# The first layer's MLP by 2x2 blocks in seven products

## The chip, the core and the metric

One NeuronCore of a Trainium2 chip runs the whole two-layer network in one launch. The metric is the device time of that launch in microseconds, the median of three runs. All arithmetic is fp32. A matrix product is split for TensorE: each operand is written as a high part (rounded to the format that TensorE multiplies) plus a low part (what is left), and three products are accumulated: high by high, high by low, low by high.

## The reference, cut to what matters

```python
for l in range(2):                       # D_MODEL 1024, D_FF 4096, 1024 latent + 256 context tokens
    ...                                  # projection, attention / convolution / Fourier heads, output projection
    x = layer_norm(ALPHA * x + g1 * mix_x, ln1_g[l], ln1_b[l])
    x = layer_norm(ALPHA * x + g2 * squared_relu_mlp(modulate(x, sh2, sc2), w_up[l], w_down[l]), ln2_g[l], ln2_b[l])
    if l == 0:
        ...                              # the same for ctx, with its own modulation vectors
def squared_relu_mlp(h, w_up, w_down):
    return jnp.square(jax.nn.relu(h @ w_up)) @ w_down
```

In the first layer latent and context tokens go through the MLP together, 1280 tokens; in the second only the 1024 latent ones do.

## The kernel before, in words

The program's order is written out by hand: each engine runs its own instructions in the order in which the Python code issues them, and waits only for data and for buffers. Loads and most stores of the MLP stand in one queue, that of SP (`load`, L193); the projections' stores stand in ScalarE's.

Buffers in SBUF: 25 tiles of 128x1280 (`s5`, tiles named a), 20 of 128x1024 (`s4`, b), two of 128x512 for the background stream's data (w) and four of 128x256 for its sums (m). A freed buffer goes to the end of a list, and a new tile takes the one that has been free longest. PSUM has eight banks of 512 columns: two tiles of three banks (`p3`, p) and two of one bank (`p1`, q).

`mm3` (L205 to L207) issues the three matmuls of one product tile. `lo` (L201) makes a low part, on VectorE or GpSimd.

Layer 0's MLP is `mlp_steps`. The hidden layer has 32 units of 128 columns. An up step `u(f)` multiplies one unit for all 1280 tokens, in chunks of 512, 512 and 256 columns: 24 matmuls each. ScalarE then makes Relu and Square (L1959, L1960), GpSimd the exact square (L1961) and VectorE the low part. A down step `d(j)` takes two units and all ten tiles of 128 tokens, two halves of 512 columns each, six matmuls a half, 120 in all, and VectorE adds the result to the sum in SBUF (L2025). The steps alternate: d, u, u, d, u, u. Units 0 and 1 are computed ahead, at the end of the output projection (`pre`). In the last down step the gate and the residual are folded into the sum (GpSimd L2043, VectorE L2046). Then comes unit 31, and `finish` does the last two units' down product with the layer norm, tile by tile (L2245).

A background stream (`stream`) is drawn on between steps: first `resid_jobs`, 20 jobs that make the residual from the stored layer-norm output (L1468, L1469), then `mod_jobs`, 16 jobs for each modulation vector that is still to come (L308, L310). A job loads 256 KB while its predecessor runs and gives two turns. Behind every fourth job stands a tail: a few small matmuls and one or two VectorE instructions on a PSUM tile. Three of the ten modulation vectors are made in `in_proj` of layer 0 (`NREST0`), the other seven in layer 0's MLP.

Layer 1's MLP is `mlp_blocks` and `down_blocks`. There the products go by 2x2 blocks in seven instead of eight products (Strassen's scheme in Winograd's form). Two units and two halves of the tokens make one pair `p`. The seven products are numbered; 1, 6, 7 and 4 accumulate in one PSUM bank, 5 and 3 in a second, 2 in a third, and between products ScalarE or VectorE reads the partial sum (`evac`, L1661 to L1674). The hidden blocks are summed (L1685), and all seven forms of them are stored to DRAM. The down phase loads them back, makes high and low parts (L1788, L1791, L201), multiplies by tiles of 128 tokens, and VectorE adds each product to the sum in SBUF (L1889). Four units are not in blocks: two done ahead, two `plain`. The token sums that the blocks need are made from fp32 copies of the MLP's input, which the output projection stores to DRAM in layer 1 (`XF`, in `to_T`). The second halves of `X2`, free by then, hold the weights' high and low parts.

Of the kernel before, what the change touches and what calls it, by code (L numbers as in the profile page):

```python
# [10 lines left out]
F32 = mybir.dt.float32  # L11
# [23 lines left out]
NREST0 = 3  # L35
# [110 lines left out]
class Prog:  # L146
    def __init__(self, nc, tc, a, out, pools):
        self.nc, self.tc, self.a, self.out = nc, tc, a, out
        self.cp, self.sp, self.ppc, self.dp = pools
        self.pp = self.ppc.__enter__()  # L150
        self.NP1 = 2
        self.n = 0
        self.wsrc, self.wrdy, self.wraw = [], [], []
# [14 lines left out]
    def s4(self, dt=F32, shape=(128, 1024)):  # L168
        return self.sp.tile(list(shape), dt, tag="s4", bufs=self.N4, name=self.nm("b"))
# [115 lines left out]
    def mod_jobs(self, idx):  # L285
# [5 lines left out]
        def job(q, kt):  # L291
            cs = slice(256 * q, 256 * q + 256)

            def load():
                w = self.sp.tile([128, 2, 256], F32, tag="mw", bufs=2, name=self.nm("w"))
# [4 lines left out]
            def run(w):  # L300
                if kt == 0:
                    acc[q] = {v: self.sp.tile([128, 256], F32, tag="ma", bufs=4, name=self.nm("m")) for v in vecs}
# [450 lines left out]
    def in_steps(self, X, l, PS):  # L753
# [11 lines left out]
        for i in range(NREST0) if l == 0 else ():  # L765
# [518 lines left out]
    def out_proj_setup(self, l):  # L1284
# [6 lines left out]
        self.XF = self.dr([KT, 128, SEQ]) if l else None  # L1291
# [154 lines left out]
    def resid_jobs(self, l, T):  # L1446
# [4 lines left out]
        def job(q, t):  # L1451
            cs = slice(512 * q, 512 * q + 512)

            def load():
                if q not in G:
                    G[q] = [[self.sp.tile([128, 256], F32, tag="ma", bufs=4, name=self.nm("m")) for _ in range(2)]
# [5 lines left out]
                w = self.sp.tile([128, 2, 256], F32, tag="mw", bufs=2, name=self.nm("w"))  # L1462
# [3 lines left out]
            def run(w):  # L1466
# [6 lines left out]
                self.nr -= 1  # L1473
# [4 lines left out]
    def mlp_seq(self, l):  # L1478
        seq = [("u", 0), ("u", 1), ("u", 2)]
        J = NFF // 2  # L1480
        for j in range(J - 1 - l):
            seq.append(("d", j))
            seq += [("u", f) for f in (2 * j + 3, 2 * j + 4) if f < NFF]
        if l:
            seq.append(("u", NFF - 1))
        return seq

    def mlp_push(self, l):
        self.WQ = 2
        if l:  # L1490
            for f in range(2 * NPL):
                self.wq_push(self.a["wu"][l, f], [128, KT, 128])
            return
# [7 lines left out]
    def mlp(self, X2, l):  # L1501
        with self.tc.manual_schedule():
            if l:
                self.mlp_blocks(X2, l)
            else:
                self.mlp_steps(X2, l)

    def mlp_blocks(self, X2, l):
# [186 lines left out]
        self.bank_pool()  # L1695
# [45 lines left out]
    def bank_pool(self):  # L1741
        self.ppc.__exit__(None, None, None)
        self.ppc = self.tc.tile_pool(name="pq", bufs=1, space=PSUM, reuse_waits="tile")
        self.pp = self.ppc.__enter__()
        self.NP1 = 8
# [623 lines left out]
```

## Time and profile before

| | |
|---|---|
| median of 3 runs | 2980.92 us (2979.51 to 2981.08) |
| the profiled execution, its span | 2984.5 us, 2982.5 us |
| busy: TensorE, VectorE, ScalarE, GpSimd | 95%, 63%, 33%, 33% |
| mean granted TensorE clock | 0.976 |
| layer 0's MLP, from unit 2 to the closing stage | 789.73 to 1650.68 us |

Times in the rows are from the span's start. PE is TensorE, PEld its weight loads, DVE is VectorE, ACT ScalarE, POOL GpSimd, SP the queue that issues most DMAs. A matmul's duration runs from its start to its modelled end, and successive ones overlap, so the rate is read from the distance of starts.

### The profile page before, as it was taken

To read this page: it belongs to the slowest core of one execution; us is meant where nothing else is said; L and a number is where in the kernel's file an instruction comes from. 1 tells how busy PE (TensorE), PEld (TensorE's weight loads), DVE (VectorE), ACT (ScalarE), POOL (GpSimd) and SP (SyncE) were. 2 spreads that over 40 slices of the span, in tenths; PEclk is the share of its full clock that TensorE was granted. 3 is DMA by queue.
4 is the path that set the end of the run, shared out by engine and by line. 5 is a ranking of instruction groups with operands and counts; after the bars stand their busy time and mean duration, and the time that the engine had idled before them with its cause. 6 is when DMAs were issued, how large, how long until landed. Compare 5 with 4: busy or idle time off the path is not lost. (4 is left out here: it accounts for less than half of the span.)

```text
span 2982.5 us, 36498 instructions
## 1 busy us (share of the span) xinstructions
PE 2821.0 (95%) x14164; PEld 2359.7 (79%) x14164; DVE 1890.7 (63%) x2725; ACT 997.4 (33%) x1364; POOL 986.9 (33%) x596
## 2 busy tenths in 40 slices
PE   7899989889999999999999899999989899999996
PEld 5788888778888878888887688888777788878875
DVE  6667768845345576655556743467855577668887
ACT  4221156523421111111111432146623555553331
POOL 2512135633211100000104640036655000058785
PEclk9999999999999999999999999999999999999998
DMA  7244652336223222223223223254345555464442
GB/s 258 82 158 135 188 131 68 103 132 215 85 85 111 78 91 90 89 82 98 80 88 124 113 87 134 94 163 94 109 146 191 176 206 196 149 232 156 155 151 96
DMA packets 197201, 389.16 MB, mean 130 GB/s; under 512 B 16702, under 2 KB 109348, under 8 KB 197028
## 3 DMA queue, kind: packets, MB, share of 16 engines
q1 hardware_dynamic: 176856, 315.47, 33.7%
q10 hardware_dynamic: 17292, 61.93, 5.4%
q0 software_dynamic: 2880, 9.44, 0.8%
q8 instruction: 111, 1.82, 0.3%
q14 instruction: 62, 0.51, 0.1%
HBM read 283.44 MB, written 103.34 MB: 130 GB/s over the span
## 5 line engine op out<-in xcount | busy, mean ns | idle before, releaser
L206 PE MATMUL p<-a,b 128*128 128x512 f32 (+1 forms) x1784 | 653.7, 366 | 1.1 <-POOL a L201 1.0
L205 PE MATMUL p<-a,b 128*128 128x512 f32 (+1 forms) x1512 | 552.1, 365 | 5.3 <-ACT b L1926 3.1
L207 PE MATMUL p<-a,b 128*128 128x256 f32 (+1 forms) x1496 | 539.2, 360 | 3.2 <-DVE b L201 3.1
L205 PE MATMUL q<-b,a 128*128 128x512 f32 (+1 forms) x1300 | 475.8, 366 | 27.9 <-ACT b L575 9.5
L206 PE MATMUL q<-b,a 128*128 128x512 f32 (+1 forms) x1300 | 469.2, 361 | 2.5 <-DVE b L201 2.5
L207 PE MATMUL q<-b,a 128*128 128x512 f32 (+1 forms) x1300 | 469.1, 361 | 0.1
L206 PEld LDWEIGHTS p<-a,b 128*128 128x128 f32 x1784 | 340.0, 191 | 52.3 <-POOL a L201 1.9
L205 PEld LDWEIGHTS p<-a,b 128*128 128x128 f32 x1512 | 287.6, 190 | 51.6 <-issue 6.2
L207 PEld LDWEIGHTS p<-a,b 128*128 128x128 f32 x1496 | 283.8, 190 | 47.8 <-DVE b L201 4.7
L205 PEld LDWEIGHTS q<-b,a 128*128 128x128 f32 x1300 | 248.5, 191 | 83.5 <-DVE b L2025 16.1
L2025 DVE TENSOR_TENSOR b<-q,b 128x512 f32<-128x512 f32 x280 | 192.6, 690 | 155.9 <-PE q L207 154.2
L206 PEld LDWEIGHTS q<-b,a 128*128 128x128 f32 x1300 | 248.5, 191 | 37.5 <-DVE b L201 3.1
L207 PEld LDWEIGHTS q<-b,a 128*128 128x128 f32 x1300 | 248.2, 191 | 37.5 <-DVE a L201 0.5
L201 DVE TENSOR_TENSOR b<-b,b 128x1024 fp32r<-128x1024 f32 (+1 forms) x119 | 181.4, 1532 | 150.4 <-ACT b L1926 119.1
L201 DVE TENSOR_TENSOR a<-a,a 128x1280 fp32r<-128x1280 f32 (+4 forms) x141 | 211.0, 1497 | 94.6 <-POOL a L1961 67.8
L1961 POOL TENSOR_TENSOR a<-a 128x1280 f32<-128x1280 f32 x31 | 72.0, 2322 | 585.6 <-ACT a L1960 585.6
L310 DVE SCALAR_TENSOR_TENSOR m<-w,k,m 128x256 f32<-128x256 f32 x448 | 226.4, 519 | 50.8 <-DMA w<-wmr 41.2
L201 POOL TENSOR_TENSOR a<-b,a 128x256 fp32r<-128x256 f32 (+2 forms) x133 | 176.8, 1339 | 241.9 <-ACT a L1791 126.1
L205 PE MATMUL q<-a,a 128*128 128x512 f32 x554 | 218.5, 394 | 14.7 <-DVE b L1889 13.1
L929 DVE TENSOR_REDUCE c<-p 128x1 f32<-128x1280 f32 x128 | 190.5, 1488 | 65.0 <-PE p L927 63.7
L207 PE MATMUL q<-a,a 128*128 128x512 f32 (+1 forms) x576 | 225.7, 392 | 0.2 <-DVE a L201 0.2
L206 PE MATMUL q<-a,a 128*128 128x512 f32 x568 | 223.7, 394 | 2.3 <-POOL a L201 2.3
(270 smaller groups left out, 4749.0 us busy)
## 6 DMA issues: line engine op xcount, KB each, us to landing
w<-wmr SPq DMA_DIRECT2D x160, 256.0 KB
a<-d SPq DMA_DIRECT2D x76, 512.0 KB
b<-wu SPq DMA_DIRECT2D x64, 512.0 KB
b<-wd SPq DMA_DIRECT2D x62, 512.0 KB
d<-a ACTq DMA_DIRECT2D x40, 640.0 KB
a<-d SPq DMA_DIRECT2D x80, 320.0 KB
d<-a SPq DMA_DIRECT2D x46, 512.0 KB
b<-wi SPq DMA_DIRECT2D x32, 512.0 KB
```

The lines of the kernel that those rows point to most:

```text
L201: (eng or self.nc.vector).tensor_tensor(out, x, hi, op=ALU.subtract)
L205: mm(out, lh, rh, start=start, stop=False, skip_group_check=on)
L206: mm(out, lh, rl, start=False, stop=False, skip_group_check=on)
L207: mm(out, ll, rh, start=False, stop=stop, skip_group_check=on)
L310: nc.vector.scalar_tensor_tensor(a, w[:, i], s, a, op0=ALU.mult, op1=ALU.add)
L929: nc.vector.reduce_max(mx, ps[:, :nkey], axis=AX.X, negate=True)
L1961: nc.gpsimd.tensor_tensor(r[:, s], r[:, s], r[:, s], op=ALU.mult)
L2025: nc.vector.tensor_tensor(a, ps, a, op=ALU.add)
```

## The change

Layer 0's MLP goes by blocks too, in a function of its own, `mlp_blocks0`, and in a common `down_blocks`. A token half has 640 columns there, so a product's moving operand is two parts of 320 columns, on a PSUM tile of two banks (`p2`, four of them). The order of the products differs from layer 1's. The down phase has five token tiles in each half, and all eight banks: five for the products 1, 6, 7 and 4, three for 5, 3 and 2. The two plain units' hidden values and those of units 0 and 1 are stored, and multiplied at the end: units 0 and 1 in `down_blocks`, 2 and 3 in `finish`. The pool of 128x1024 tiles is divided anew for the up phase: five `s4`, twelve 128x1280 tiles `t5`, and the stream's tiles; afterwards it has its 20 tiles again. Layer 0's output projection now stores `XF` too. Four of the modulation vectors (64 jobs, of one vector each) move from layer 0's MLP to `in_proj` of layer 1.

```diff
-NREST0 = 3
+NREST0, NREST1 = 3, 6
+BKU = {1: 2, 2: 1, 3: 1, 4: 2, 5: 1, 6: 1, 7: 2}
...
+    def p2(self):
+        return self.pp.tile([128, 2, 512], F32, tag="p2", bufs=4, name=self.nm("q"))
...
-        for i in range(NREST0) if l == 0 else ():
+        for i in range(NREST0) if l == 0 else range(NREST1, len(REST)):
             jobs += self.mod_jobs(i)
...
-        self.XF = self.dr([KT, 128, SEQ]) if l else None
+        self.XF = self.dr([KT, 128, SEQ if l else TOK])
...
+    def mlp_blocks0(self, X2, l):
...
+        self.sbuf(5)
+        self.anchor = self.last_load
+        jobs = self.resid_jobs(l, T)
+        for i in range(NREST0, NREST1):
+            jobs += self.mod_jobs(i)
+        bg = self.stream(jobs)
...
+        def plain_evac(f, ps):
+            r = self.t5()
+            act.activation(r, ps[:, :n], AF.Relu)
+            act.activation(r, r, AF.Square)
+            return lambda: self.load(self.HL[f], r)
...
+        def sum_split(k):
+            TS[k] = []
+            for j, x in enumerate(S1.pop(k)):
+                hi, lo = [(self.t5 if j and (k or i) else self.s5)(F32R) for i in range(2)]
+                act.copy(hi, x)
+                self.lo(lo, x, hi)
+                TS[k].append((hi, lo))
...
+        seq = [(NPL, 1), (NPL, 2)]
+        for p in range(NPL, NP):
+            seq += [(p, 5), (p, 6)] + [(p, 2)] * (p > NPL) + [(p, 7), (p, 3)]
+            seq += [(p + 1, 1)] * (p < NP - 1) + [(p, 4)]
...
+        def prod(n, o, start):
+            hi, lo = F.pop(n)
+            i = seq[n][1]
+            for h in range(2):
+                c = slice(Q2 * h, Q2 * h + Q2)
+                for k in range(4):
+                    xh, xl = B[i](k)
+                    self.mm3(o[:, h, :Q2], hi[:, k], lo[:, k], xh[:, c], xl[:, c], start and k == 0, k == 3, not start)
...
+        def evac(n):
...
+            if i in (1, 6):
+                act.copy(two(h["q"][:, int(i == 6)]), ps)
+            elif i == 7:
+                y = h["r"][:, 1]
+                act.copy(two(y), ps)
+                c = Q[p][5][:, :, :Q2]
+                return lambda: v.tensor_tensor(two(y), c, two(y), op=ALU.add), lambda: square(y)
+            elif i == 2:
+                y = h["q"][:, 0]
+                v.tensor_tensor(two(y), ps, two(y), op=ALU.add)
+            elif i == 4:
+                y = h["r"][:, 0]
+                act.activation(two(y), ps, AF.Relu)
+                Q.pop(p)
+                return None, lambda: act.activation(y, y, AF.Square)
+            elif i == 3:
+                y = h["q"][:, 1]
+                v.tensor_tensor(two(y), ps, two(y), op=ALU.add)
+            return None, None if y is None else (lambda: square(y))
...
+        st = [plain_evac(f, ready[f]) for f in range(2)]
+        pconv(2)
+        sum_load(0)
+        st.append(plain(2, {0: [P(sum_add, 0), P(pconv, 3)], 1: [st[0], P(sum_load, 1), P(sum_split, 0)],
+                            2: [st[1], P(wload, NPL), P(sum_add, 1)], 3: [P(sum_split, 1), P(sum_load, 2), back],
+                            4: [P(sum_add, 2), back], 5: [P(sum_split, 2), P(sum_load, 3)]}))
+        st.append(plain(3, {0: [P(sum_add, 3)], 1: [P(sum_split, 3), st[2], P(wload, NPL + 1)], 2: [back], 3: [back],
+                            4: [back], 5: [back]}))
+
+        self.psum(0)
...
+        for k, (p, i) in enumerate(seq):
+            q = Q.setdefault(p, {})
+            q[i] = q[{6: 1, 7: 1, 4: 1, 3: 5}[i]] if i in (6, 7, 4, 3) else self.p2()
+            prod(k, q[i], i in (1, 2, 5))
+            nxt = evac(k)
+            whi(k + 3)
+            wlo(k + 2)
+            if nxt[0]:
+                nxt[0]()
+            wsum(k + 4)
+            if post:
+                post()
+            post = nxt[1]
...
+            if i == 6 and p > NPL:
+                hstore(p - 1)
+            if i == 3:
+                wload(p + 2)
+            if i == 7:
+                tail()
+            if i == 4:
+                tail()
+            back(BKU[i])
+            if p == NP - 1 and i in (2, 7, 3):
+                next(down)
+        post()
...
     def down_blocks(self, l, NG):
...
+        order, steps = ((1, 5, 6, 3, 2, 7, 4), [(i, t) for i in (1, 5, 6, 3, 2, 7, 4) for t in al]) if l else (
+            (1, 5, 3, 6, 2, 7, 4),
+            [(i, t) for i, ts in ((1, al), (5, (0, 1, 2)), (3, (0, 1, 2)), (5, (3, 4)), (6, (0, 1)), (3, (3, 4)),
+                                  (6, (2, 3, 4)), (2, al), (7, al), (4, al)) for t in ts])
...
+        def where(i, t):
+            if i in (1, 6, 7, 4):
+                return "x", t
+            if l:
+                return "y", t
+            return "y", (t % 3 if i != 2 else (t + 2) % 3)
...
+        tasks = {0: [P(hraw, 2), P(wl, 2)], 1: [P(wl, 3)], 2: [hconv, P(hraw, 3)], 3: [wm], 4: [hconv], 5: [wm],
+                 T - 1: [P(fold_late, T + i) for i in range(FL)]}
+        for t in range(T):
+            c = slice(128 * t, 128 * t + 128)
+            for m in range(2):
+                ps = (bk["x"] + bk["y"])[(2 * t + m) % 8]
+                evac(2, ps)
+                d = slice(NB * m, NB * m + NB)
+                for e in range(2):
+                    self.mm3(ps, H[e][0][:, c], H[e][1][:, c], W[e][0][:, d], W[e][1][:, d], e == 0, e == 1)
+                evq.append((acc[t][:, d], ps, False))
+            evac(0)
+            fold_late(t)
+            for f in tasks.get(t, ()):
+                f()
...
-    def mlp_steps(self, X2, l):
...
-        wraw(NFF - 2)
-        wraw(NFF - 1)
+        wraw(2)
+        wraw(3)
```

`whi` and `wlo` make a weight block's high part (ScalarE) and low part (VectorE), `wsum` the sum of two blocks (VectorE), `hsums` the four sums of hidden blocks (VectorE), `back` takes one turn of the background stream, and `tail` one step of a modulation tail.

## Rows read from the trace of the kernel before

**Rows 1.** The page, part 1: busy time, share of the span, instructions.
```profile
PE 2821.0 (95%) x14164; PEld 2359.7 (79%) x14164; DVE 1890.7 (63%) x2725; ACT 997.4 (33%) x1364; POOL 986.9 (33%) x596
```
**Rows 2.** Table by stage: window, length, busy time by engine, clock, DMA share, GB/s.
```profile
789.73:1650.68 860.95, 852.89 (x4093) 704.81 (x4092) 505.76 (x830) 148.92 (x145) 122.41 (x65) 1.00 0.29 91
1597.92:1650.68 52.76, 45.43 (x201) 35.92 (x200) 40.91 (x36) 6.96 (x8) 41.66 (x15) 0.97 0.39 133
1655.00:1682.00 27.00, 18.94 (x81) 12.77 (x80) 26.24 (x40) 10.13 (x10) 15.10 (x11) 1.00 0.24 96
2327.00:2340.00 13.00, 9.82 (x34) 7.30 (x33) 8.88 (x11) 5.96 (x6) 0.00 (x0) 0.74 0.88 334
2375.00:2580.00 205.00, 202.68 (x889) 166.42 (x889) 141.22 (x250) 106.72 (x190) 8.79 (x16) 1.00 0.56 191
1740.00:2000.00 260.00, 252.40 (x1471) 223.52 (x1470) 122.93 (x112) 69.68 (x86) 48.66 (x28) 0.99 0.37 120
```
**Rows 3.** Instructions in order of time, layer 0's MLP, TensorE: start, duration, operation.
```profile
858.94 0.40 PE L205 MATMUL q<-b,a 128*128 128x512 f32 x1
...
886.54 0.39 PE L205 MATMUL p<-a,b 128*128 128x512 f32 x1
...
897.42 0.28 PE L205 MATMUL p<-a,b 128*128 128x256 f32 x1
...
900.29 0.40 PE L205 MATMUL p<-a,b 128*128 128x512 f32 x1
```
**Rows 4.** Groups by line, VectorE, layer 1's up phase: count, busy, mean ns, idle before.
```profile
L201 DVE TENSOR_TENSOR a<-b,a 128x512 fp32r<-128x512 f32 x52 | 35.5, 685 | 1.6 <-ACT a L1634 1.2
...
L1469 DVE TENSOR_TENSOR w<-w,m 128x256 f32<-128x256 f32 x31 | 13.2, 425 | 1.1
...
L1674 DVE TENSOR_TENSOR a<-q,a 128x512 f32<-128x512 f32 x11 | 7.6, 692 | 27.5 <-PE q L207 27.5
```
**Rows 5.** Groups by line, VectorE, layer 0's MLP.
```profile
L310 DVE SCALAR_TENSOR_TENSOR m<-w,k,m 128x256 f32<-128x256 f32 x280 | 132.6, 483 | 35.7 <-DMA w<-wmr 29.6
...
L201 DVE TENSOR_TENSOR a<-a,a 128x1280 fp32r<-128x1280 f32 x27 | 40.2, 1488 | 67.8 <-POOL a L1961 67.8
```
**Rows 6.** Groups by line, ScalarE, layer 1's up phase: a copy from PSUM.
```profile
L1661 ACT COPY a<-q 128x512 f32<-128x512 f32 x22 | 13.0, 589 | 25.2 <-PE q L207 25.2
```
**Rows 7.** Groups by line, ScalarE, layer 0's MLP: Relu from PSUM.
```profile
L1959 ACT ACTIVATE a<-p 128x1280 f32<-128x1280 f32 x28 | 34.8, 1242 | 322.1 <-PE p L207 322.1
```
**Rows 8.** In order of time, layer 1's last pair, product 7 and 4 behind it.
```profile
2623.37 0.39 PE L207 MATMUL q<-b,a 128*128 128x512 f32 x1
2623.80 0.59 ACT L1663 COPY a<-q 128x512 f32<-128x512 f32 x1 [3.81 <-PE q L207]
...
2624.44 0.50 PE L205 MATMUL q<-b,a 128*128 128x512 f32 x1 [0.68 <-ACT a L1663]
```
**Rows 9.** In order of time, start of layer 1's MLP, TensorE.
```profile
2327.23 0.28 PE L207 MATMUL p<-a,b 128*128 128x256 f32 x1
2330.65 0.79 PE L205 MATMUL p<-a,b 128*128 128x512 f32 x1 [3.14 <-ACT b L1926]
...
2358.26 0.50 PE L205 MATMUL q<-a 128*128 128x512 f32 x1 [2.71 <-ACT a L1634]
```
**Rows 10.** In order of time, layer 1, first down product, TensorE.
```profile
2631.73 0.49 PE L205 MATMUL q<-a,a 128*128 128x512 f32 x1 [1.55 <-ACT a L1791]
...
2634.31 0.79 PE L206 MATMUL q<-a,a 128*128 128x512 f32 x1 [2.08 <-POOL a L201]
```
**Rows 11.** Groups by line, VectorE, layer 1's down phase.
```profile
L201 DVE TENSOR_TENSOR a<-a,a 128x1024 fp32r<-128x1024 f32 x34 | 67.1, 1973 | 2.4 <-ACT a L1788 2.4
```
**Rows 12.** In order of time, end of layer 0's MLP: GpSimd's folds, first closing add.
```profile
1621.66 16.64 POOL L2043 TENSOR_TENSOR b<-b,b 128x1024 f32<-128x1024 f32 x5 [1.34 <-DVE b L2025]
...
1651.58 0.69 DVE L2245 TENSOR_TENSOR b<-q,b 128x512 f32<-128x512 f32 x1 [1.20 <-PE q L207]
```
**Rows 13.** Groups by line, VectorE, in_proj of layer 0.
```profile
L310 DVE SCALAR_TENSOR_TENSOR m<-w,k,m 128x256 f32<-128x256 f32 x152 | 83.6, 573 | 14.7 <-DMA w<-wmr 11.6
```

More of the change, by code (lines that the diff above doesn't have):

```diff
@@ L1455, in load @@
                 if q not in G:
-                    G[q] = [[self.sp.tile([128, 256], F32, tag="ma", bufs=4, name=self.nm("m")) for _ in range(2)]
+                    G[q] = [[self.ma() for _ in range(2)]
                             for _ in range(2)]
@@ L1505, in mlp @@
             else:
[L1506 removed]
+                self.mlp_blocks0(X2, l)
     def mlp_blocks(self, X2, l):
@@ L1753, in down_blocks @@
         seq = [(n, i) for n in range(NG) for i in order]
+        prods = [(n, i, t) for n in range(NG) for i, t in steps]
         acc = [None] * T
@@ L1819, in loads_to @@
                 pos[0] += 1
-        for k in (2, 4, 5):
-            loads_to(k)
-            yield
+        if l:
+            for k in (2, 4, 5):
+                loads_to(k)
+                yield
+        else:
+            for k in (3, 4):
+                loads_to(k)
+                yield
         f = form(*seq[0])
@@ L1830, in down_blocks @@
         yield
-        loads_to(7)
+        loads_to(7 if l else 6)
         for _ in form(*seq[1]):
             pass
-        bk = {b: [self.p1() for _ in range(4)] for b in "xy"}
-        W, H, S = [], [], []
+        self.psum(8)
+        bk = {"x": [self.p1() for _ in al], "y": [self.p1() for _ in range(8 - TH)]}
+        W, H, S, HR = [], [], [], []
         xr = {}
         self.acc = acc
+        gate = lambda t: self.gs[int(t >= 8)][:, :D]
         def rload(t):
@@ L1889, in evac @@
                     v.tensor_tensor(a, ps, a, op=ALU.add)
[L1891 to L1908 removed]
+        fm = iter(())
@@ new lines, in down_blocks @@
+        for k, (n_, i, t) in enumerate(prods):
+            if k % TH == 0:
+                for _ in fm:
+                    pass
+                j = k // TH + 2
+                fm = iter(())
+                if j < len(seq):
+                    loads_to(11 * seq[j][0] + need[seq[j][1]] + 4)
+                    fm = form(*seq[j])
+            b, w = where(i, t)
+            ps = bk[b][w]
+            evac(2, ps)
+            prod(n_, i, t, ps, i in (1, 5, 2))
+            r, c = to[i]
+            if acc[t + TH * r] is None:
+                acc[t + TH * r] = self.s4()
+            evq.append((acc[t + TH * r][:, NB * c:NB * c + NB], ps, n_ == 0 and first.get(i) == (r, c)))
+            evac(2)
+            next(fm, None)
+            if k in tail:
+                tail[k]()
+            if k == 7 and l:
```

517 lines of the change are left out of this document (253 added, 264 removed).

## The prediction

> **What bounds the kernel now.** I read the page's busy line first: TensorE is busy 95% of the span and nothing else comes near [rows 1]. Then the table by stage: the first layer's MLP, from the first plain matmul after the two units computed ahead (789.73) to the first matmul of the closing stage (1650.68), is 860.95 us long with TensorE busy 852.9 of it, at full clock, and VectorE 505.8 [rows 2]. So in this stage time is matmul columns, and fewer columns are time, as long as nothing else comes to end last. Matmul durations overlap, so the cost of one is the distance of starts: 48 matmuls of 512 columns go from 886.54 to 897.42, 0.2267 us each, and 24 of 256 from 897.42 to 900.29, 0.1196 us each [rows 3]. A line through both gives 0.1464 us for 320 columns (in proportion to the 512 it would be 0.1417, to the 256 0.1495).
>
> **What is saved.** A plain up unit is 13.75 us [rows 3]; 28 of the 32 become blocks: 14 pairs of 7 products of 24 matmuls of 320 columns, 2352 x 0.1464 = 344.3 us instead of 385.0: -40.7 (between -52 and -33 by the two proportions). A plain down step (a pair of units) is 120 x 0.2267 = 27.2 us; 14 become 7 groups of 7 x 5 x 6 = 210 matmuls, 47.6 each: 333.2 instead of 380.8, -47.6. Gross: -88.3.
>
> **What the up phase gives back.** The order inside a pair is 5, 6, 2, 7, 3, next pair's 1, 4. Product 3 accumulates on the PSUM tile of product 5, and evac of 7 reads that tile on VectorE after ScalarE has copied product 7. So TensorE must stop between 7 and 3 in every pair. Layer 1 has this dependency with two products in between, and its up phase is busy 202.7 of 205 us [rows 2]; here nothing stands between. The price: where layer 1 has the first half of this chain once (its last pair), the last matmul began at 2623.37, so the next was due at 2623.60; ScalarE's copy began at 2623.80 and TensorE restarted at 2624.44, right behind the copy [rows 8]. That is 0.20 us to notice, the copy, and some 0.05. A 640-column copy lies between 0.589 (512) and 1.242 (1280): 0.70 [rows 6, 7]. The VectorE add of 640 from PSUM is 0.692 [rows 4] plus 128 columns by the line of 0.425 and 0.685 us for 256 and 512: 0.82. So 0.20 + 0.70 + 0.03 + 0.82 + 0.02, and 0.1 for the slower first matmul: 1.88 us, 14 times, 26.3. Half of the twelve modulation tails' small matmuls fall into the gaps: -3. The first pair has 6 and 7 next to each other as well: +1. Net +24. Bounds: 9 (only the copy's half) to 45 (VectorE late by as much again).
>
> Would VectorE end last? Per pair it has 4 weight sums and 7 low parts of 512 (11 x 0.685 = 7.5), 3 adds from PSUM (2.5), 4 hidden-block sums of 640 (4 x 0.815 = 3.3) [rows 4] and 10 background halves of two instructions of 0.43 to 0.48 (9.5) [rows 4, 5]: 22.8 of the 24.6 + 1.9 = 26.5 us of TensorE. It fits, with 3.7 us to spare, most of it just ahead of evac 2 and evac 7. A low part is made two products ahead, which leaves 1.8 us or more for each. PSUM slots: four two-bank tiles, three per pair, the longest free one is taken, so a new 5 gets one that has long been read; I charge nothing, and 1 us per pair if it were the one just finished.
>
> **Start.** Layer 1's block MLP has plain_evac of both ready units in ScalarE's queue ahead of the conversion of the third unit's weights; so has the new one, where the old one converted first and lost nothing. In layer 1 TensorE went from 2327.23 (+0.12) to 2330.65 without work [rows 9], 3.3 us, and came back at the lower clock: the mean granted is 0.74 over the 13 us around it [rows 2]. [...]
>
> Ahead of the first product VectorE must have done, after this: two weight low parts (2.4), 16 sums of 640 (13.0), 8 low parts of 1280 (8 x 1.488 [rows 5] = 11.9), 6 background halves (5.7), 2 sums and 1 low part of 512 (2.1): 35.1 us, and 3 to 4 us of pauses until ScalarE has copied each sum. [...]
>
> **Between the phases.** After the last product ScalarE has Relu of 4, Relu and Square of 3, Square of 4 and the first down weight's copy (0.2 + 0.7 + 1.5 + 0.75 + 1.0 = 4.2 us, by the line through 0.59 for 512 and 1.24 for 1280 columns [rows 6, 7]), then GpSimd's low part, some 2.4. Layer 1 waited 1.55 and 2.08 there and started its next matmuls slow (0.79) [rows 10]. I take 6.4 + 3: +9.4 (5 to 16, if the redivided buffers make ScalarE wait for a store).
>
> **Down phase.** Per product (5 tiles, 6.8 us) VectorE has 5 adds of 0.69 and a low part of 1280. With GpSimd at work the 1024 one took 1.97 [rows 11], so some 2.45: 5.9 us, 87%, as busy as layer 1 was. But three banks instead of four now carry products 5, 3 and 2, so a bank comes back after three tiles (4.08 us), and a low part and two adds in a row take 3.85. +5 (0 to 12).
>
> **End.** Before, the last down step with its folds and unit 31 took 52.76 us for 41.0 of matmuls, TensorE idle through GpSimd's five multiplications in 16.64 us [rows 2, 12], and the closing stage's first add came at 1651.58. Now the folds lie in the last plain step (units 0, 1), GpSimd has 10 x 3.3 + 2 low parts (6.6) = 40 us behind the first tile, and no up unit follows to let it catch up: some 45 us for 27.2. Lost 17.8 instead of 11.8: +6 (0 to 12).
>
> **Moved work.** The four second-layer jobs that leave the MLP go to in_proj of layer 1, with 16 of the 28 tails' matmuls, as long there as here: 0. VectorE was 47% busy there in all (122.9 of 260 [rows 2]), and 64 jobs of 2 instructions add some 65 us; but a job has two turns, 128, and I count 113 turns in that unit order. The other 15 run in a row behind the last unit, some 12 us on VectorE in front of the attention, partly behind the V units: +7 (0 to 15). In layer 0 the same loop waited 11.6 us for weights in 152 instructions [rows 13]. The 20 new XF stores sit on SP's queue ahead of the output projection's loads: +2 (0 to 6).
>
> **Sum.** -88.3 + 24 + 6.7 + 11 + 9.4 + 5 + 6 + 7 + 2 = -17.2. Block steps also have no tails in the down phase, where a plain step with such work took 27.6 us (858.94 to 886.54 [rows 3]) instead of 27.2: -2. So -19 on 2984.5 of the profiled execution (span 2982.5): 2965.5; the median shown is 3.6 below that execution: 2962.
>
> **Rivals.**
> (1) The stop between 7 and 3 is not there or is half as long (the add gets ahead, or tails and clock effects are smaller), and start and transition are as cheap as in layer 1: -12 to -15 for the first, -12 for the others: 2936. For it: layer 1 runs this scheme almost without idle. Against it: its order, which is another.
> (2) VectorE becomes the bound of the up phase, by late background loads. It has 3.7 us to spare per pair; each of the 5 jobs per pair waits for a 256 KB load that stands on SP behind stores and weight loads. In in_proj of layer 0 the wait was 11.6 us over 152 instructions, four to a job [rows 13]: 0.3 us a job, 1.5 a pair, within it. From 1.0 us a job on, the gain of 19 is gone (5.1 - 3.7 = 1.4 a pair, 19 in 14); at 1.5 us a job it is 14 x 3.8 = 53, 34 more than the gain: 3015, slower.
> (3) The stops make the clock swing. The closing stage has stops of 1.3 to 1.9 us every 5 us and its granted clock is 1.00, TensorE busy 18.9 of 27 [rows 2]: against it. [...]
> (4) Several givebacks at their upper ends: no change, 2980.
>
> **Chances.** The forecast's case 0.55, 2948 to 2975 by itself; (1) 0.20; (4) 0.13; (2) 0.08; (3) 0.04. What a measurement of this kernel can tell from no change is 0.2%, 6 us. The range from 2930 to 2986 takes in the first, (1) and (4), and leaves out (2), (3) and what is better than (1). Faster 0.74, same 0.13, slower 0.13.
>
> **What would show it.** After the change: in the up phase, TensorE idle 1.3 to 1.9 us ahead of a matmul of 320 columns 14 times, released by VectorE's add in evac, at full clock, and starts of 320-column matmuls 0.146 apart; one restart at the lower clock after the ready units, one ahead of the first product, one between the phases; VectorE at 84 to 90% in the up phase; a down group of 48 to 49 us. Wrong: no idle at 7 to 3, or one of over 3 us; a DMA ahead of VectorE's background instructions for over 1 us each; an up phase of more than 385 us or under 350.

## The result, and the profile after

The changed kernel takes 3015.22 us (3014.33 to 3019.86) against 2981.00 of the kernel before on the same chip: 1.0118 times as long, 95% interval 1.0100 to 1.0135. It is slower; the prediction said 2962 us and faster. The profiled execution took 3015.05 us, its span is 3013.3, 30.8 more than before.

TensorE has fewer columns to do, and is busy for less of a longer span, which answers to [rows 1]:

```profile
PE 2749.9 (91%) x14290; PEld 2349.5 (78%) x14290; DVE 2068.2 (69%) x2926; ACT 1153.4 (38%) x1610; POOL 1127.3 (37%) x642
```

So the question is where it stands. The table by stage (window, length, busy time of TensorE, its weight loads, VectorE, ScalarE, GpSimd, each with a count, then clock, DMA share, GB/s), in order: up phase of layer 0's MLP from the first block matmul, down phase, last plain down step to the first matmul of layer 1's in_proj, that in_proj's units, and what lies between its last unit and V1 (the second half of the V projection, ten tiles of 24 matmuls, which the code issues behind all units):

```profile
823.75:1224.30 400.55, 367.04 (x2432) 359.43 (x2433) 284.30 (x545) 159.13 (x254) 10.27 (x19) 0.97 0.50 172
1224.30:1577.83 353.53, 342.00 (x1470) 278.93 (x1471) 276.17 (x279) 124.63 (x121) 212.04 (x78) 0.98 0.44 158
1577.83:1673.83 96.00, 68.32 (x273) 52.97 (x272) 72.49 (x99) 21.91 (x23) 64.74 (x33) 0.84 0.20 77
1673.83:1940.41 266.58, 258.32 (x1414) 219.36 (x1413) 158.51 (x216) 72.86 (x91) 66.21 (x56) 0.99 0.45 152
1940.41:1981.69 41.28, 3.31 (x18) 3.14 (x16) 18.03 (x32) 4.37 (x4) 3.38 (x1) 0.53 0.72 206
```

The kernel before had no such last row. Its in_proj's units took 258.12 us, and V1's first matmul followed the last unit's after 0.22 us (1950.43, 1950.65). The same units in the kernel before:

```profile
1692.53:1950.65 258.12, 251.97 (x1381) 218.50 (x1380) 109.25 (x96) 74.06 (x92) 66.04 (x56) 0.99 0.34 112
```

The first matmul of in_proj came at 1692.53 before and comes at 1673.83 now, 18.7 us earlier. Not all of that is the MLP's. Unit 2 was due at 785.55 here and began at 789.73 before, 4.2 us apart, and the two executions had already drifted apart in layer 0's attention, which the change leaves alone; in the kernels with the new MLP unit 2 begins anywhere from 786.0 to 791.9. From where unit 2 was due, the first layer's MLP gained 14.5 us, with a new stop at its start in it:

```profile
789.27 0.60 PE L234 MATMUL p<-a,b 128*128 128x512 f32 x1 [3.56 <-ACT b L1833]
```

V1's first came at 1950.65 and comes at 1981.69: 31.0 lost. So in_proj lost 49.7: 8.5 in its units and 41.3 behind them (rounded); from V1 on both kernels take the same time (to the last matmul 1014.0 before, 1013.6 after).

TensorE at that stop, the small matmuls alone, in order of time (start, duration, operation, count, in brackets the idle time before and what ended it):

```profile
1940.41 0.50 PE L386 MATMUL q<-k,m 128*128 128x2 f32 x4
1958.66 0.98 PE L386 MATMUL q<-k,m 128*128 128x2 f32 x4 [17.75 <-DVE m L339]
1973.20 0.98 PE L386 MATMUL q<-k,m 128*128 128x2 f32 x4 [13.56 <-DVE k L399]
1980.84 0.98 PE L386 MATMUL q<-k,m 128*128 128x2 f32 x4 [6.66 <-DVE k L399]
```

VectorE in the same stretch:

```profile
1940.40 1.22 DVE L570 TENSOR_TENSOR a<-a,b 128x1024 f32<-128x1024 f32 x1
1954.05 1.23 DVE L230 TENSOR_TENSOR b<-b,b 128x1024 fp32r<-128x1024 f32 x1 [12.44 <-ACT b L2280]
...
1968.02 2.04 DVE L339 SCALAR_TENSOR_TENSOR m<-w,k,m 128x256 f32<-128x256 f32 x4
1972.05 1.01 DVE L339 SCALAR_TENSOR_TENSOR m<-w,k,m 128x256 f32<-128x256 f32 x2 [1.99 <-DMA w<-wmr]
```

SP's queue, from the last stretch of the units on:

```profile
1918.12 14.30 SPq L222 DMA_DIRECT2D w<-wmr  x5
1932.52 8.60 SPq L222 DMA_DIRECT2D a<-d  x12
1942.19 0.35 SPq L222 DMA_DIRECT2D b<-wv  x1
1943.65 33.54 SPq L222 DMA_DIRECT2D w<-wmr  x10
```

Read them together. When the last unit ends, ten of the 64 moved jobs are left (the ten loads in the last row). The code runs them to the end, and the tails behind them, before it issues V1. So three tails of four tiny matmuls (L386) stand in TensorE's queue ahead of V1's 240 and wait for sums (L339) that VectorE makes from 1955 to 1981. (Two of the rows name L399, a small VectorE instruction that reads an earlier tail's PSUM tile; it ends within 0.1 us of the sums, so the rows can't tell the two apart.) VectorE itself first waits 12.44 us for the conversion of V1's second weight block: SP issues that load only at 1942.19, behind twelve loads for the first attention head and five job loads that took 14.30 us. Each of the five waits for a buffer: of SP's waits there 6.8 us end with VectorE's sums and 4.7 with the landing of an earlier job load. V1's weights were ready at 1955.3, its first matmul came 26 us later (1981.69), behind the third tail (1980.84), as they were issued. Whether it could have run ahead of the tails is not shown, for a second thing held V1: tails and V1's tiles take the same two one-bank PSUM tiles in turn, and the one that V1's first tile takes was read (L399) only at 1980.61. Both follow from the order of issue, and no run here separates them.

### The profile page after: what moved, and what is told of

Read it like the earlier page. It is cut to its first block, busy times and chain, and to the rows that moved or that the text cites. A ratio compares the mean times of both kernels' runs of the same rounds, so it can differ in the third digit from the quotient of the medians.

```text
span 3013.3 us, 37703 instructions
## 1 busy us (share of the span) xinstructions
PE 2749.9 (91%) x14290; PEld 2349.5 (78%) x14290; DVE 2068.2 (69%) x2926; ACT 1153.4 (38%) x1610; POOL 1127.3 (37%) x642
## 5 line engine op out<-in xcount | busy, mean ns | idle before, releaser
L234 PE MATMUL q<-a,a 128*128 128x512 f32 (+1 forms) x1632 | 599.0, 367 | 53.8 <-DVE t L1931 26.7
L236 PE MATMUL q<-a,a 128*128 128x512 f32 (+2 forms) x1682 | 611.5, 364 | 3.2 <-DVE a L230 3.2
L235 PE MATMUL q<-a,a 128*128 128x512 f32 (+1 forms) x1618 | 591.7, 366 | 5.5 <-POOL a L230 5.5
L235 PE MATMUL p<-a,b 128*128 128x512 f32 (+1 forms) x1088 | 407.1, 374 | 1.1 <-POOL a L230 1.0
L234 PEld LDWEIGHTS q<-a,a 128*128 128x128 f32 x1632 | 311.2, 191 | 107.0 <-DVE t L1931 30.5
L230 POOL TENSOR_TENSOR a<-b,a 128x256 fp32r<-128x256 f32 (+2 forms) x163 | 249.2, 1539 | 331.8 <-ACT a L2081 156.4
L236 PEld LDWEIGHTS q<-a,a 128*128 128x128 f32 x1682 | 320.4, 190 | 47.0 <-DVE a L230 4.7
L235 PEld LDWEIGHTS q<-a,a 128*128 128x128 f32 x1618 | 309.0, 191 | 48.4 <-POOL a L230 6.7
L2217 DVE TENSOR_TENSOR b<-q,b 128x512 f32<-128x512 f32 x425 | 279.2, 684 | 95.7 <-PE q L236 95.2
L230 DVE TENSOR_TENSOR a<-a,a 128x1280 fp32r<-128x1280 f32 (+4 forms) x156 | 290.1, 1860 | 43.2 <-ACT a L2078 31.8
L234 PE MATMUL p<-a,b 128*128 128x512 f32 (+1 forms) x816 | 305.2, 374 | 7.5 <-ACT b L1833 3.6
L236 PE MATMUL p<-a,b 128*128 128x512 f32 (+1 forms) x800 | 293.1, 366 | 3.9 <-DVE b L230 3.9
L234 PE MATMUL q<-b,a 128*128 128x256 f32 (+1 forms) x740 | 255.9, 346 | 41.0 <-DVE b L2217 15.8
L230 POOL TENSOR_TENSOR a<-a,a 128x1024 fp32r<-128x1024 f32 (+2 forms) x49 | 134.0, 2737 | 399.6 <-ACT a L2081 330.5
L339 DVE SCALAR_TENSOR_TENSOR m<-w,k,m 128x256 f32<-128x256 f32 x448 | 228.8, 523 | 48.1 <-DMA w<-wmr 38.8
L236 PE MATMUL q<-b,a 128*128 128x256 f32 (+1 forms) x740 | 252.6, 341 | 0.6 <-DVE a L230 0.6
L235 PE MATMUL q<-b,a 128*128 128x256 f32 (+1 forms) x740 | 252.7, 342 | 0.0
L235 PEld LDWEIGHTS p<-a,b 128*128 128x128 f32 x1088 | 208.2, 191 | 33.9 <-POOL a L230 1.9
L989 ACT ACTIVATE a<-p,c 128x1280 f32<-128x1280 f32 x128 | 170.5, 1332 | 90.0 <-DVE c L958 82.6
L234 PEld LDWEIGHTS q<-b,a 128*128 128x128 f32 x740 | 144.7, 196 | 64.4 <-DVE b L2397 14.6
L234 PEld LDWEIGHTS p<-a,b 128*128 128x128 f32 x816 | 156.2, 191 | 34.3 <-issue 4.7
```

What stands on the lines that cost most here:

```text
L230: (eng or self.nc.vector).tensor_tensor(out, x, hi, op=ALU.subtract)
L234: mm(out, lh, rh, start=start, stop=False, skip_group_check=on)
L235: mm(out, lh, rl, start=False, stop=False, skip_group_check=on)
L236: mm(out, ll, rh, start=False, stop=stop, skip_group_check=on)
L339: nc.vector.scalar_tensor_tensor(a, w[:, i], s, a, op0=ALU.mult, op1=ALU.add)
L989: self.nc.scalar.activation(e[:, :nkey], ps[:, :nkey], AF.Exp, bias=mx, accum_out=s)
```

## The experiments

M is the theory that the moved jobs are the loss. Its rival B: the redivided buffers, or the new MLP, slow what follows.

**One part left out, and one part alone.** The changed kernel without the four moved jobs:

```diff
-        for i in range(NREST0) if l == 0 else range(NREST1, len(REST)):
+        for i in range(NREST0) if l == 0 else ():
...
```

> The changed kernel with the four second-layer modulation jobs left out altogether (their vectors are taken from the first layer's). Theory M (moved work): the 41.3 us in which TensorE stands between the last unit and V1 of the second layer's in_proj, and 8.4 us lost during its units, are the four jobs; without them 3015 - 50 = 2965 us, and the stretch from the first Fourier unit to V1 takes 261 us as before. Rival B (buffers): the redivided SBUF and PSUM, not the jobs, slow what follows the first layer's MLP; then the stretch stays at 308 us or so and the time over 3000.

2961.22 us, 0.9929 of before (0.9916 to 0.9943). And the kernel before with only the move:

```diff
-        for i in range(NREST0) if l == 0 else ():
+        self.tailp = self.p1
+        for i in range(NREST0) if l == 0 else range(6, len(REST)):
...
-            for i in range(NREST0, len(REST)):
+            for i in range(NREST0, 6):
```

> The kernel before with nothing changed but that the four second-layer jobs run in the second layer's in_proj. Theory M: 40 to 50 us are lost there, up to 5 are gained in the first layer's MLP, which has fewer tails: 3016 to 3026 us. Rival B: without the redivided buffers the move costs what the prediction took, +7 or less: 2976 to 2988 us.

3026.21 us, 1.0148 of before (1.0132 to 1.0165). The table's row for in_proj's units without the jobs:

```profile
1670.46:1926.49 256.03, 250.23 (x1381) 216.88 (x1379) 109.02 (x96) 73.91 (x92) 65.75 (x56) 0.99 0.34 113
```

The kernel before with the move, TensorE:

```profile
1970.22 0.98 PE L357 MATMUL q<-k,m 128*128 128x2 f32 x4 [17.68 <-DVE m L310]
1984.88 0.99 PE L357 MATMUL q<-k,m 128*128 128x2 f32 x4 [13.69 <-DVE k L370]
1992.32 0.99 PE L357 MATMUL q<-k,m 128*128 128x2 f32 x4 [6.45 <-DVE k L370]
```

The same three waits stand in a kernel with the old MLP and the old buffers, and none where the jobs are left out. B is out as the cause of the loss, M is shown.

**More turns at each hook**, so that no job is left over (`slot(3 if l else BGK)`).

> The changed kernel with three background turns at each hook of the second layer's in_proj instead of two, so that no job is left over behind the last unit. Theory M1 (the left-over jobs in a row are the stop, as their tails' matmuls stand ahead of V1 in TensorE's queue): the 41.3 us stop falls to under 5 and the units lose some us more: 2974 to 2982 us. Rival M2 (the loads: the unit weights stand on SP's queue behind job loads that wait for VectorE, so denser jobs make the weights later): TensorE waits for weights inside the units instead, 20 us or more in sum, 2995 us or more.

3002.75 us, 1.0070 of before (1.0055 to 1.0084): the time is in the rival's range. Its mechanism holds only in part. The stop is gone, but the units now take 285.84 us instead of 266.58, and the first score matmul of the attention comes 15.0 us behind V1's first instead of 8.4. TensorE's longest waits from the first unit into the attention (total, times, longest):

```profile
PE q L386 <- DVE m L339: 6.5, 3, 4.8
PE q L234 <- ACT b L604: 6.3, 5, 4.5
PE q L234 <- ACT b L2280: 5.2, 1, 5.2
```

The largest is not for weights, as the rival had it, but for the jobs' sums, in tails; one of 5.2 is for V1's weights (L2280), and the waits for ScalarE's copy out of PSUM (L604) the rival did not name. The mean clock over these units is 0.96 instead of 0.99.

**The left-over jobs between V1's tiles**, three turns behind each:

```diff
...
+        def v1():
+            for _ in self.vproj(X, l, 1):
+                for _ in range(3):
+                    next(bg, None)
+                tail()
+                yield
+            rest()
...
```

`rest` runs what is left to its end, as the code did ahead of V1 before.

> The changed kernel; the jobs left over behind the last unit of the second layer's in_proj are not run ahead of V1 but between V1's token tiles, three turns behind each. Theory O (order in TensorE's queue): most of the 41.3 us stop is tails' matmuls that stand ahead of V1 and wait for VectorE's sums; what is left is V1's second weight block, which is issued at 1942.2 and was converted by 1955: a stop of 13 to 15 us, and VectorE's 10 us of sums are hidden in the attention: 3015 - 27 = 2988, with 2 for the tails 2990. Rival L (VectorE or the loads are the bound, wherever the jobs stand): the attention's row maxima wait behind the sums, and 15 us or more come back there: 3003 us or more.

2999.00 us, 1.0062 of before (1.0049 to 1.0074), between the two. The three waits for VectorE ahead of V1 are gone; one comes in their place, for the second weight block, within V1:

```profile
1956.33 0.58 PE L234 MATMUL q<-b,a 128*128 128x256 f32 x1 [12.21 <-ACT b L2294]
```

So the order of issue is worth 40 us up to V1's first matmul, but not that much in all: from there to the last matmul it is now 1036.7 us instead of 1013.6. Of these 23.1 the wait is 12.2; the rest wasn't taken apart.

**A third buffer for the jobs' weights** (`tag="mw", bufs=3`), alone and with the jobs between V1's tiles:

> The changed kernel with three buffers for the background jobs' weights instead of two, nothing else. Theory Q (SP's queue): with two slots SP stands at a job's load until VectorE is through with the job two back, and what is behind it on SP (V1's weights, the next loads) comes late; a third slot takes VectorE's 29 us of waits for job loads in the second layer's in_proj to under 10 and its 12.4 us wait for V1's weights to under 4, so the stop ahead of V1 falls from 41.3 to 20 to 25: 2993 to 2999 us. Rival O2: the stop is the order alone (tails ahead of V1, ten jobs in a row on VectorE): it stays over 35 us and the time over 3008.

> Third slot and left-over jobs between V1's tiles. Theories O and Q together: no stop ahead of V1 (under 3 us), the 12.2 us wait for V1's second weight block gone, what remains of the moved work are 16 tails (about 8 us) and some late row maxima: 2981 to 2988 us. Rival L: VectorE's sums delay the attention whatever the loads do: no more than 5 us below the run without the third slot, 2994 us or more.

3009.50 us, 1.0095 (1.0078 to 1.0111), and 2989.08, 1.0032 (1.0020 to 1.0045). VectorE's waits for job loads in in_proj fell as expected, from 29.0 us (23.5 and 5.5) to 9.3:

```profile
DVE m L339 <- DMA w<-wmr: 7.4, 6, 2.5
DVE m L337 <- DMA w<-wmr: 1.9, 2, 1.0
```

but the stop ahead of V1 only from 41.3 to 35.1, and VectorE's wait for V1's second block stayed at 12.5, since that block was issued at 1935.00 for a last unit that ended at 1935.2, only 2 us sooner relative to it. By stop and time the first run is rival O2's: theory Q was wrong in that part. SP issued its loads in program order here too (five job loads in 12.44 us, then the head's twelve, then V1's), so with one buffer more it was one job further ahead, not free. The second run lies between its two ranges; its wait for that block is still 9.4.

**V1's second block ahead of the head's loads**, on the third buffer, the jobs between V1's tiles and the other product order (below):

```diff
             if i == len(units) - 2:
+                while l and self.wsrc:
+                    self.wload()
                 self.heads = {0: self.head_load(0, l)}
```

> Third slot, left-over jobs between V1's tiles, the order 5, 6, 2, 7, next 1, 3, 4, and V1's second weight block issued on SP ahead of the twelve loads for the first attention head, not behind them. Theory Q2 (place on SP): the 9.6 us wait ahead of V1 goes, and with it some 3 us of matmuls at the lower clock: 2955 to 2961 us. Rival: the head's loads, later by the same time, hold the attention's first score matmul, or VectorE is the bound there: 2964 us or more.

2972.26 us, 0.9963 of before (0.9952 to 0.9974), in the rival's range and not told apart from 0.9958 without it. The wait did not go, it moved. VectorE, in order of time:

```profile
1911.10 1.23 DVE L230 TENSOR_TENSOR b<-b,b 128x1024 fp32r<-128x1024 f32 x1 [2.32 <-ACT b L2296]
1923.49 1.00 DVE L339 SCALAR_TENSOR_TENSOR m<-w,k,m 128x256 f32<-128x256 f32 x2 [11.16 <-DMA w<-wmr]
```

And TensorE:

```profile
1927.64 0.58 PE L234 MATMUL q<-b,a 128*128 128x256 f32 x1 [13.68 <-ACT b L604]
```

Now VectorE stands at a job load, which is behind the head's twelve loads, and ScalarE, whose next work needs VectorE, is late in emptying V1's PSUM. What stood behind those twelve came late in both runs (VectorE's waits of 12.44 us for V1's block and of 11.16 for this job load); no run here spreads them.

**Fewer jobs moved.** Two jobs stay in the first layer's up phase, `NREST1 = 8` and `BKU` 2 for every product (so 14 turns a pair, not the 13 that the expectations name):

> The changed kernel with only two of the four second-layer jobs moved (64 turns, which fit in in_proj's 108 or so), the other two stay in the first layer's up phase with 13 turns a pair instead of 10. Theory M: no job is left over in in_proj, and its 49.9 us shrink to 4 to 6 (tails of 0.36 us, one wait): -44; the up phase gets 8 more tails of 0.6 (+5) and 2.2 us more of VectorE a pair, which fits in its idle quarter (+0 to +6): 2976 to 2982 us. Rival D (the prediction's second rival: VectorE becomes the bound of the up phase): 15 us or more are lost there: 2988 us or more.

3027.19 us, 1.0155 of before (1.0141 to 1.0169): rival D. In in_proj the theory held: V1's first matmul comes 266.3 us after in_proj's first, instead of 307.9, without a stop. The up phase lost more than that. The same kernel without the job loads, all modulation sums taken from one tile loaded once:

> Two jobs moved, two more in the first layer's up phase (13 turns a pair), with the sums of all of the MLP's modulation jobs taken from one weight tile loaded once, so that VectorE's work is the same and the job loads are gone (the modulation vectors are other ones). Theory W (late loads hold VectorE, which then is late for the add of 7): the up phase falls from 445.6 us to 400 to 412 and the time from 3027 to under 2995. Rival V (VectorE's own work, in its order ahead of the add, is too much): the up phase stays over 430 us, the time over 3010.

3001.85 us, 1.0067 of before (1.0054 to 1.0080). And the changed kernel with none of these jobs in either place:

> The changed kernel with all modulation jobs behind the first layer's in_proj left out (three of the first layer's MLP, four of the second layer's in_proj; other vectors are used in their place); the residual's background work stays. It shows the block scheme by itself. Theory U (the up phase's 390.5 us instead of the 368 forecast are the tails' matmuls, a VectorE that comes late behind background sums, and the spells at the lower clock behind longer stops): 14 stops of 1.95 between starts, no spell at the lower clock but the first, 370 to 374 us from the first block product at full speed to the last; in all 2938 to 2945 us. Rival P (the products themselves are slower than forecast, or the stop is longer without any other work): the up phase stays above 382 us and the time above 2950.

2952.33 us, 0.9908 of before (0.9894 to 0.9922). The up phase of the three, from its first block matmul to the first down matmul, in the order of the text; the changed kernel's is the first row of the table above, 400.55:

```profile
823.57:1273.23 449.66, 387.47 (x2448) 375.62 (x2448) 314.08 (x617) 160.80 (x254) 10.32 (x19) 0.92 0.52 172
```

without the loads:

```profile
826.00:1244.65 418.65, 376.84 (x2448) 365.19 (x2448) 313.72 (x617) 159.80 (x254) 10.28 (x19) 0.96 0.39 134
```

with no jobs:

```profile
823.99:1212.86 388.87, 354.17 (x2353) 349.56 (x2353) 200.84 (x325) 158.16 (x254) 10.27 (x19) 0.98 0.42 144
```

What jobs cost is not in proportion to their own time. With none the phase takes 388.9 us. The changed kernel's 48 are 83.5 us of VectorE's time (284.30 less 200.84) and cost 11.7. 32 more, of one vector each, are 29.8 and cost 49.1; of those 31.0 go when the loads of all 80 go, though VectorE's busy time is the same (314.08, 313.72). VectorE's longest waits from 831 to 1269 with the loads (L339 and L337 are for job loads, L1497 for the residual's):

```profile
DVE m L339 <- DMA w<-wmr: 26.0, 15, 2.4
DVE w L1497 <- DMA w<-d: 17.6, 7, 4.9
DVE t L1934 <- PE q L236: 15.7, 5, 5.1
DVE m L337 <- DMA w<-wmr: 9.8, 3, 4.8
```

They make VectorE late for the add of product 7: TensorE's 14 stops there are 52.3 us instead of 26.7, the longest 9.0. Theory W holds for most of it, not for all: without loads the phase is still 18.1 above the changed kernel's (414.6 to its last matmul, where 400 to 412 were expected). Theory U holds for half: without any modulation job the products take 378.6 us from 830.2 on, 390.2 in the changed kernel, where 370 to 374 were expected, and the time is over the 2938 to 2945 expected. The 14 stops are 27.1 us there too: thirteen have the forecast size, and one of 6.0 stands behind a VectorE that waits 4.6 us for a load of the residual's. A third buffer with the loads in place:

> Two jobs moved, two kept in the first layer's up phase (13 turns a pair), with the third slot. With two slots that up phase took 445.6 us against 396.5, VectorE waiting 31.5 us for job loads. Theory W (late loads): with the third slot VectorE's waits fall under 8 us, and the up phase to 400 to 412 us: 2984 to 2996 us. Rival V (VectorE's own 82 to 85% of work is too dense ahead of the add of 7): the up phase stays over 430 us and the time over 3012.

3016.17 us, 1.0124 of before (1.0107 to 1.0141), the phase 438.5 by the expectation's measure, and VectorE's waits for job loads 31.1 us still up to 1215 (24.0 and 7.1): rival V by the numbers, but with the loads as late as before. So the jobs' own buffer was not all that they waited for. SP's queue shows what else: its waits in this phase that end with VectorE's low parts of weights (L230; the loads of the next weight blocks stand there) and hidden sums (L1953; their stores), with two buffers

```profile
SPq L222 <- DVE a L230: 80.4, 13, 8.3
SPq L222 <- DVE t L1953: 47.7, 16, 4.6
```

and with three:

```profile
SPq L222 <- DVE a L230: 116.4, 20, 12.8
SPq L222 <- DVE t L1953: 67.6, 17, 6.6
```

The waits that end with job sums (L339) fell from 95.2 to 40.2. The job loads stand on SP behind those weight loads and stores, which now wait longer. That this is what makes them late is read from the queue; no run takes the weights and stores off it.

**The stop between products 7 and 3.** The next pair's product 1 in between:

```diff
-            seq += [(p, 5), (p, 6)] + [(p, 2)] * (p > NPL) + [(p, 7), (p, 3)]
-            seq += [(p + 1, 1)] * (p < NP - 1) + [(p, 4)]
+            seq += [(p, 5), (p, 6)] + [(p, 2)] * (p > NPL) + [(p, 7)]
+            seq += [(p + 1, 1)] * (p < NP - 1) + [(p, 3), (p, 4)]
```

> The changed kernel with the order 5, 6, 2, 7, next pair's 1, 3, 4 in the first layer's up phase, so that 24 matmuls stand between product 7 and product 3. Theory S (the stop is the copy of 7 and the add that reads 5's tile): the 26.7 us in 14 stops fall to under 4: 2988 to 2992 us. Rival V: VectorE or a PSUM tile's release ends last anyway, the stop moves to another product: under 10 us gained, 3005 us or more.

3011.81 us, 1.0102 of before (1.0083 to 1.0120): rival V. in_proj began 10.6 earlier (1663.26 instead of 1673.83), and the up phase takes 390.7 us instead of 400.55, not 26 less: the stop went, and VectorE's low parts of weights ended last in its place. The two largest of TensorE's waits that changed:

```profile
PE q L236 <- DVE a L230: 11.4, 12, 3.0
...
PE q L234 <- DVE t L1931: 4.8, 2, 3.1
```

The same order on top of the run with two jobs moved gave 3016.87 us, 1.0122 of before (1.0107 to 1.0138), 10.3 below that run. The 8 to 10 us less that were expected came; the 2967 to 2973 us, which took that run for 2976 to 2982, did not.

With the third buffer and the jobs between V1's tiles the same order is worth more:

> As before, and the order 5, 6, 2, 7, next 1, 3, 4 in the first layer's up phase. If the order is worth what it was alone in the first layer's MLP (8 to 10 us by the start of in_proj), 2972 to 2980 us; if VectorE's lateness eats it, as above.

2967.47 us, 0.9958 of before (0.9944 to 0.9972), 22 below the same without it, where 2972 to 2980 was expected; the up phase (as above) takes 379.20 us, not 400. So the third buffer alone is worth next to nothing in this phase (399.2 us instead of 400.55), the order alone 9.9, both together 21.4. With the third buffer VectorE waits 5.8 us for the residual's loads there, not 26.6, and TensorE 6.8 for low parts (L230), not 11.4; that is part of the difference, the rest is not accounted for.

**The end.** The last plain step's weights scaled by the gate on VectorE instead of GpSimd, on top of V1's weights first:

> As e13, and in the first layer's last plain down step the two closing weight blocks are scaled by the gate on VectorE instead of GpSimd. If VectorE's two waits of 8.5 us for the scaled weights (with the adds that free PSUM behind them) are what makes TensorE stop for 13.7 and 6.6 us there, 6 to 12 us less than e13. If GpSimd's ten multiplications by the gate are the bound (24 us and the two low parts of 3.9), under 4 us less.

2963.80 us, 0.9951 of before (0.9938 to 0.9965), on the same chip 8.5 below. From the step to in_proj it is 88.77 us instead of 93.94, 5.2; the rest of the difference is not accounted for, and the two intervals overlap. The time is in the theory's range, its mechanism is not borne out: VectorE's two waits went (17.1 us in all, now 2.2), but TensorE's long stops, 13.7 and 6.6 before, hardly moved:

```profile
1594.49 0.76 PE L234 MATMUL q<-b,a 128*128 128x512 f32 x1 [12.59 <-DVE b L2233]
1605.44 0.79 PE L234 MATMUL q<-b,a 128*128 128x512 f32 x1 [6.42 <-DVE b L2413]
```

This has the lowest ratio of the runs that do all the work, but noise does not tell it from 0.9958 and 0.9963.

## Why the prediction was wrong

**The step that failed** is "Moved work": 16 tails "0", and +7 (0 to 15) for 15 left-over turns "partly behind the V units". The count was nearly right (ten jobs are twenty turns), the cover was not there. In program order V1 is issued behind the drain, and its first matmul came behind the drain's third tail (1981.69, 1980.84), so its matmuls covered nothing; I had taken TensorE's next work for independent without asking what stood in its queue ahead of it. Nor is the drain 12 us of VectorE: it is VectorE in its own order, behind the wait for V1's weights, which the same jobs had made late on SP. Forecast 7, measured 49.7; with the jobs left out, the kernel is 54 us faster by the times, and the move alone costs the old kernel 43. Without it 2961 us stand against a forecast of 2955 (2962 less the 7). That they are so near is partly luck: the MLP's own terms were off in both directions.

**The MLP's terms**, in this execution (the sum up to in_proj: -28 forecast without the moved work and the stores; -18.2 measured from unit 2's first matmul on, -14.5 with the stop ahead of it):

| term | forecast | measured |
|---|---|---|
| both restarts ahead of the first block product | +17.7 | +10.9, and 3.7 ahead of unit 2 |
| up: 28 units' time against 385.0 | -16.7 | +7.7 |
| between the phases | +9.4 | 3.9, and 3 behind the first down matmul |
| down against 380.8 | -42.6 | -27.3, the 3 included |
| end | +6 | +15.1 |
| what the plain steps took beyond their bare matmuls, which goes | -2 | -28.6 |

Start: the +6.7 and the +11 of the sum were my estimates of two stops, each with slower matmuls behind it. No run shows these terms; in their place the trace shows the following. TensorE stood 3.7 us ahead of unit 2, from 785.55 to 789.27. Ahead of the first block product stood these two, 7.8 us, and from 827.69 the products ran:

```profile
823.75 0.63 PE L234 MATMUL q<-a 128*128 128x320 f32 x1 [4.71 <-ACT a L1894]
824.18 0.47 PE L235 MATMUL q<-a,a 128*128 128x320 f32 x1
827.69 0.63 PE L236 MATMUL q<-a,a 128*128 128x320 f32 x1 [3.04 <-DVE a L230]
```

Slower matmuls behind these stops cost 3.1 us up to 827.69 (granted clock 0.55 from 789.27 to 792.00, 0.50 from 823.75 to 827.69), and another 2.8 behind it (0.50 up to 833.90), which stand in the next row of the table.

Up, from 827.69 to 1220.39: the 320-column matmul was right, 2256 starts lie 0.1466 us apart on average (0.1464 forecast): 344.8. The stop was right as a mechanism and nearly in size, here one of them, TensorE and then ScalarE and VectorE:

```profile
989.48 0.31 PE L236 MATMUL q<-t,a 128*128 128x320 f32 x1
991.43 0.41 PE L234 MATMUL q<-a,a 128*128 128x320 f32 x1 [1.64 <-DVE t L1931]
```

ScalarE:

```profile
989.82 0.69 ACT L1929 COPY t<-q 128x640 f32<-128x640 f32 x1 [5.31 <-PE q L236]
```

VectorE:

```profile
990.55 0.82 DVE L1931 TENSOR_TENSOR t<-q,t 128x640 f32<-128x640 f32 x1 [1.30 <-ACT t L1929]
```

The next matmul was due at 989.63, the copy took 0.69 (0.70 forecast), the add 0.82 (0.82), TensorE stood 1.80 (1.88). But four of the fourteen were 2.4 to 6.3, where VectorE came late or a tail stood in between: 32.4 us in all, not 26.3. Of the eleven tails in this stretch two fell into a stop and cost nothing, two stood in stops of 2.8 and 3.0, and seven cost 0.8 to 1.05 each beside them: +6.3, where I had assumed -3 for half of them. And 71 matmuls lie 0.22 to 0.43 apart, 48 of them in three spells at a granted clock of 0.50 or 0.51, behind the start and behind stops of 6.3 and 2.8: with one wait of 0.8, +9. So the up phase is over the 385 us that I had named as a sign of being wrong; VectorE, which I had put at 84 to 90% there, was busy for 71% (284.30 of 400.55).

Down: 1470 x 0.2267 = 333.2 are there; 16.7 us more instead of 5 were lost, in nine waits for a bank (5.2 us), one for ScalarE's first copies (3.3) and slower matmuls behind them (granted clock 0.50 from 1244.80 to 1250.20, behind the 3.3). VectorE, which I had put at 87% there, as busy as in layer 1, was busy for 78% (276.17 of 353.53), and in layer 1 for 80% from 2631.73 to 2880.00 (197.64 of 248.27). End: GpSimd was the cause I named. The trace shows VectorE standing 17.1 us in two waits at a low part of weights that GpSimd has not scaled, with the adds behind it that free PSUM; but the last experiment took these waits away and 5.2 us with them, so the larger part of the +15.1 stays open:

```profile
1589.52 1.85 DVE L2161 SCALAR_TENSOR_TENSOR b<-a,b 128x1024 f32<-128x1024 f32 x1
1599.98 1.22 DVE L230 TENSOR_TENSOR b<-a,b 128x1024 fp32r<-128x1024 f32 x1 [8.61 <-ACT b L2174]
1601.12 1.28 DVE L2217 TENSOR_TENSOR b<-q,b 128x512 f32<-128x512 f32 x2
```

The last line of the table saved the rest. Units 2 to 30 and 14 down steps took 808.2 us before (789.73 to 1597.92 [rows 2]), 28.6 more than 29 x 13.75 + 14 x 27.2. From the first tiny matmul of a tail to the next large one it is 17.0 us of that, in 27 tails; the rest lies in 512-column matmuls a little further apart (0.230 us on average). I had compared the blocks with bare plain steps and read the -2 from a single step.

**The rivals.** Rival (2), VectorE as the bound of the up phase by late loads, gave 3015, the very time; it is not what happened here, but with 32 jobs more it is. VectorE's waits for job loads are 3.9 us in the whole up phase; for the residual's loads they are 23.0 in eight, of which one, 4.2 us long, lies ahead of the 6.3 us stop. Rival (3): behind a stop of 1.80 the first two matmuls lie 0.25 apart and the next ones 0.15, and the granted clock from 900 to 1100 is 1.00, so the stops of this size did not make the clock swing. Behind the stop of 6.3 (0.50 from 881.73 to 885.10) and the one of 2.8 (0.51 from 1158.10 to 1161.50) the clock did fall, behind the one of 3.0 it did not (1.00 from 1046.80 to 1050.00), and in the kernel with two jobs moved, with stops of up to 9.0 us, it was 0.92 over the phase.

## What to carry to other kernels

Background work was not free here where foreground work stood behind it in a queue: the ten jobs ahead of V1 came with a stop of 41.3 us. Before it is moved, list for each engine and for SP what is issued next behind it, above all where the background runs out and is drained. A load that waited for its buffer held the loads behind it on SP (14.30 us ahead of V1's weights), so the price of a dense background appeared in other data that came late. And a gain is to be measured against the steps as they ran, tails and all, not against their bare matmuls.

## What the runs showed of the hardware

A modulation tail cost TensorE 0.36 us (four matmuls of 2 columns) or 0.61 us (two of 2 rows by 256) between two 512-column matmuls of in_proj: twelve of them took 8.5 us of its units, 2.1 of it a wait. VectorE at 70% busy in the up phase (314.08 of 449.66) held TensorE up at product 7 for twice as long (52.3 us) as at 71% (284.30 of 400.55, 26.7 us): its busy share says little of whether it is in time.
